# State-space blocks: one multiply for all tables, scans over four joined rows, and a later load of the gate bias

## The chip, the cores and the metric

The kernel runs on one core of a Trainium2 chip. Its engines are TensorE (PE in the profile; its weight loads are PEld), VectorE (DVE), ScalarE (ACT), GpSimd (POOL) and SyncE (SP), which here only starts DMA transfers. The metric is device time in microseconds (us); less is better.

## The reference

Two layers, one after the other, over 256 frames of width 2048. Each layer does this:

```
proj = x @ w_in                       # 2048 x 4096: q, k, v, u
attn = differential chunk-causal attention(q, k, v), 8 heads, normed per head
bu   = u @ B                          # per group of 16 channels: 64 complex states
h[t] = a * h[t-1] + bu[t]             # complex, |a| and angle per state, t = 0..255
y    = Re(C h) + d * u;  y = gelu(y)
ssm  = y * sigmoid(y @ glu_w + glu_b), normed per group
x    = layer_norm(alpha * x + concat(attn, ssm) @ w_out)
x    = layer_norm(alpha * x + relu(x @ w_up)^2 @ w_down)
```

There are 64 groups of 64 states. The change lies in the recurrence `h`, in the gelu behind it, and in where the gate's bias `glu_b` is loaded.

## The kernel before

**Matrix products.** Every large product is done three times in split fp32: weights arrive as 512 KB tiles `w` (two 128-row parts by 512 columns), ACT rounds one into `wh` (L185, by the helper on L155), DVE makes the rest `wl = w - wh` (L188, by the helper on L136), and PE multiplies hi by hi, hi by lo and lo by hi (L202). There are 714 such tiles, six buffers for `w` and four each for `wh` and `wl`.

**The mixer.** In each layer the projections, the attention heads, the state-space blocks, the gate and the output products run interleaved. A small planner (`Flow`) steps a clock of its own through tasks and writes out the order of PE's instructions; SP's order is the order in which the transfers are written. The order on DVE, ACT and POOL is chosen by the framework's list scheduler from its own model of times. So on the chip every engine works through a fixed list, and an instruction whose input is late holds up all that stand behind it on its engine.

**A state-space block** takes eight groups (four pairs `r`, two groups on the 128 partitions). Time is folded by two (`LC`), so a row has `NK` = 128 steps. There are eight blocks in a layer, 16 in all. For one block, POOL builds the tables `tab` (cosine and sine of the rotating angle, from `turn_on`, with products in `tm`), PE computes `X` = (real, imaginary) of the inputs, two pairs at a time into PSUM (L540), and DVE (`ssm_in`) turns X by the tables, scans the real and the imaginary part with the constant magnitude `magL`, and turns back. PE then forms `Y` from `h` (L581, behind the direct term of L572), and `ssm_out` applies the gelu on DVE and ACT. The tiles `wk` hold the four products, four buffers of 128x512. The planner puts the matmuls of Y `L_SCAN` = 12.5 us of its own clock behind those of X.

**Other tiles that the change touches.** `lb` (parameters B) and `ang` (angles) share the `wk` buffers during parameter preparation. `glub` is a tile of its own; its transfer stands on SP's queue among the first loads in the first layer (L1025) and ahead of the mixer in the second (L865). The pool `unit` has 18 tiles of 4 KB (`tile4k`), which nearly all other activations share.

Of the kernel before, what the change touches and what calls it, by code (L numbers as in the profile page):

```python
# [13 lines left out]
ALU = mybir.AluOpType  # L14
# [21 lines left out]
WB = 4  # L36
UN = 18
WS = 6
WK = 4
CHUNK = 64  # L40
ALPHA = (2.0 * DEPTH) ** 0.25
EPS = 1e-5
# [74 lines left out]
def trunk(ctx: ExitStack, tc: tile.TileContext, x, w_in, lambda_q1, lambda_k1, lambda_q2, lambda_k2,  # L117
# [51 lines left out]
    two = const.tile([P, 8], F32, name="two")  # L169
    for m in range(8):  # L170
        G.memset(two[:, m:m + 1], 2.0 ** m)
    mhalf = const.tile([P, 8], F32, name="mhalf")
    G.memset(mhalf, -0.5)

# [137 lines left out]
    def load_params(l):  # L312
        raw = ssm.tile([96, P], F32, tag="k0", name="prm", bufs=2)
        SY.dma_start(out=raw[0:32], in_=ssm_lambda_re[l].rearrange("(q g) p -> q (g p)", g=2))
        SY.dma_start(out=raw[32:64], in_=ssm_lambda_im[l].rearrange("(q g) p -> q (g p)", g=2))
        ld = ssm.tile([96, 2], F32, tag="ld", name="ld")
        SY.dma_start(out=ld[64:96], in_=ssm_log_dt[l].rearrange("(q g) -> q g", g=2))
        vec = ssm.tile([32, P], F32, tag="k0", name="vec", bufs=2)
        for i, v in enumerate((attn_norm_g, ssm_norm_g)):
            SY.dma_start(out=vec[8 * i:8 * i + 8], in_=v[l].rearrange("(b p) -> b p", p=P))  # L320
        for j in range(LC):
            SY.dma_start(out=vec[16:32].rearrange("x (r j c) -> x r j c", r=2, j=LC)[:, :, j],
                         in_=ssm_d[l].rearrange("(x r c) -> x r c", r=2, c=32))
        yield
        lb = [ssm.tile([P, NP_, GC], F32, tag="wk", name="lb", bufs=WK) for _ in range(2)]
        for a, v in zip(lb, (ssm_b_re, ssm_b_im)):
            SY.dma_start(out=a, in_=v[l].rearrange("(q g) p c -> (g p) q c", g=2))
            yield
        lc = [tile4k([P, 8, 2, HD], F32, "lc") for _ in range(2)]
        for i, v in enumerate((ssm_c_re, ssm_c_im)):  # L330
            for g in range(2):
                SY.dma_start(out=lc[i][:, :, g], in_=v[l].rearrange("(b g) c p -> (g c) b p", g=8))
                yield
        lq = ssm.tile([P, 4, HD], F32, tag="abc", name="lq")
        for i, v in enumerate((lambda_q1, lambda_k1, lambda_q2, lambda_k2)):
            SY.dma_start(out=lq[:, i], in_=v[l].partition_broadcast(P))
        return raw, ld, vec, lq, lb, lc

    def lay_params(fl, p, l, loaded):
# [26 lines left out]
        mag = t32("mag")[:, 0]  # L366
        G.tensor_tensor(out=mag, in0=ebase[:, 0:32], in1=tmp[:, 0], op=ALU.pow)

        rm, n = (ssm.tile([P, 8, NP_], F32, tag="wk", name="ang", bufs=WK) for _ in range(2))
        mul(rm, th.unsqueeze(1).to_broadcast([P, 8, NP_]), two.unsqueeze(2).to_broadcast([P, 8, NP_]))  # L370
        magic = 12582912.0
        ts(n, rm, 1.0 / (2.0 * math.pi), ALU.mult, magic, ALU.add)
# [33 lines left out]


        base_b, base_c = (tile4k([P, 2, NP_, GC], F32, "base") for _ in range(2))
        t1 = [ssm.tile([P, NP_, GC], F32, tag="wk", name="lb", bufs=WK) for _ in range(2)]
        for i in range(2):  # L410
            for h in range(2):
                yield fl.slot("tp")
# [5 lines left out]
                       v[64 * g:64 * g + 64, :, g], 1.0 - 2.0 * i, ALU.mult)  # L418
                give(L_EVAC)
        for o, (u, w, op) in enumerate(((0, 1, ALU.subtract), (1, 0, ALU.add))):  # L420
            mul(t1[0], lb[0], f[:, u].unsqueeze(2).to_broadcast([P, NP_, GC]))
            mul(t1[1], lb[1], f[:, w].unsqueeze(2).to_broadcast([P, NP_, GC]))
            tt_(base_b[:, o], t1[0], t1[1], op)
        p["base"], p["ab"] = (base_b, base_c), ab


# [100 lines left out]
    def ssm_in(fl, p, q, b, u):  # L527

        bT, k0, cx, tab, ready = q
        yield lambda: fl.now >= ready  # L530
        m1, m2, m3, m4 = (ssm.tile([P, 4, NK], F32, tag="wk", name="wk", bufs=WK) for _ in range(4))
        cos, sin = tab[:, 0], tab[:, 1]
        for hf in range(2):
            yield fl.slot("sx", 2)
            give = [fl.take("sx") for _ in range(2)]
            Xs = [ps_s.tile([P, 2, NK], F32, tag="sx", name="X") for _ in range(2)]
            for ri in range(2):
                for r, X in enumerate(Xs):
                    rows = slice(64 * r, 64 * r + 64)
                    TE.matmul(out=X[:, ri], lhsT=bT[rows, 2 * ri + hf], rhs=u[rows, hf], start=True, stop=True)  # L540
            fl.now += 0.87
            for r, X in enumerate(Xs, 2 * hf):
                mul(m1[:, r], X[:, 0], cos[:, r])
                mul(m2[:, r], X[:, 1], sin[:, r])
                mul(m3[:, r], X[:, 1], cos[:, r])
                mul(m4[:, r], X[:, 0], sin[:, r])
            for k, g in enumerate(give):
                g(L_X + 0.8 * k)
        add(m1, m1, m2)
        sub(m3, m3, m4)  # L550
        for g, s in ((m2, m1), (m4, m3)):
            for r in range(4):
                ml = p["magL"][:, 4 * b + r:4 * b + r + 1].to_broadcast([P, NK])
                V.tensor_tensor_scan(out=g[:, r], data0=ml, data1=s[:, r], initial=0.0,  # L554
                                     op0=ALU.mult, op1=ALU.add)
        mul(m1, m2, cos)
        mul(m3, m4, sin)
        sub(m1, m1, m3)
        mul(m2, m2, sin)
        mul(m4, m4, cos)  # L560
        add(m2, m2, m4)
        return m1, m2

    def ssm_out(fl, p, q, b, u, h):

        bT, k0, cx, tab, _ = q
        yield fl.slot("sx")
        give = fl.take("sx")
        Y = ps_s.tile([P, 2, NK], F32, tag="sx", name="Y")
        for hf in range(2):  # L570
            for r in range(2):
                TE.matmul(out=Y[64 * r:64 * r + 32, hf], lhsT=k0[:, hf, r], rhs=u[:, hf],  # L572
                          start=True, stop=False, skip_group_check=True)
            for ri in range(2):
                for i in (1, 0):
                    for r in range(2):
                        d, e = Y[64 * r + 32 * i:64 * r + 32 * i + 32, hf], h[ri][:, 2 * hf + r]
                        if i == 0:

                            d, e = d[:, 1:NK], e[:, 0:NK - 1]  # L580
                        TE.matmul(out=d, lhsT=cx[:, 2 * i + ri, 2 * hf + r].rearrange("p g c -> p (g c)"), rhs=e,  # L581
                                  start=(i == 1 and ri == 0), stop=(ri == 1), skip_group_check=True)
        fl.now += 1.5
        y, y2 = (ssm.tile([P, T], F32, tag="ge", name="ge", bufs=2) for _ in range(2))
        for hf in range(2):
            stt(y[:, hf * NK:(hf + 1) * NK], u[:, hf], p["vec"][:, 16 + 2 * b + hf:17 + 2 * b + hf], Y[:, hf],
                ALU.mult, ALU.add)
        give(L_EVAC)
        act(y2, y, AF.Square)
        ts(y2, y2, 0.044715, ALU.mult, 1.0, ALU.add)  # L590
        mul(y2, y2, y)
        act(y2, y2, AF.Tanh, scale=math.sqrt(2.0 / math.pi))
        stt(u.rearrange("p h k -> p (h k)"), y2, 1.0, y, ALU.add, ALU.mult)

# [260 lines left out]
    def mixer(l, p, xT, first):  # L855
# [4 lines left out]
        y_ev, mA_ev, mS_ev, (projected, g_ev) = events(8), events(8), events(2), events(2)  # L860
        uT = [tile4k([P, 8, NK], F32, "uT") for _ in range(2)]
        kT, qT, v = [None, None], [None, None], [None, None]
        gb = ssm.tile([P, SW], F32, tag="glub", name="glub")
        if l > 0:
            SY.dma_start(out=gb, in_=glu_b[l].partition_broadcast(P))  # L865
        loaded = []
        mA = [None, None]
        mS, glu_in, st = [], [], []
# [79 lines left out]
        def glu_inputs():  # L948
            yield both(*y_ev, projected)

            for i in range(2):
                st.append(tile4k([P, LC, NB], F32, "s"))
                for g in range(2):
                    yield fl.slot("tp")
                    give = fl.take("tp")
                    ps = transpose4(lambda n: uT[i][:, 4 * g + n])
                    fl.now += 0.44
                    act(st[i][:, :, 256 * g:256 * g + 256].rearrange("p j (x c) -> p j x c", c=32),
                        ps.rearrange("p n (r j c) -> p j (n r) c", r=2, j=LC))
                    give(L_EVAC)  # L960
            gS = Split("gS", 2)
            for i in range(2):
                for g in range(2):
# [49 lines left out]
        def main():  # L1013
            if l == 0:
                for i, test in enumerate(kproj(0)):
                    if i == 3:
                        with tc.manual_schedule(engines={ENG.Activation, ENG.DVE}):
                            turn_x(1)
                            first_w.append(wpair(w_in[0], 6, AW))
                        fl.now += 1.76  # L1020
                        for _ in range(5):
                            next(loading)
                    if i == 16:
                        loaded.append((yield from steps(loading, 0.0)))
                        SY.dma_start(out=gb, in_=glu_b[l].partition_broadcast(P))  # L1025
                    yield test
            else:
                yield from kproj(0)
# [105 lines left out]
```

## Time and profile before

| | |
|---|---|
| median of 3 runs | 2312.05 us (2311.9 to 2314.99) |
| the profiled execution | 2316.09 us |
| its span, first to last instruction | 2314.4 us |
| mean granted TensorE clock | 0.978 of full speed |

The profiled execution is 4.0 us above the median. All durations below are of this one execution. 1.7 us lie outside its span. The mixer of the first layer fills about 44 to 450 us of the span, that of the second 1180 to 1560; the MLP products lie between and behind them.

### The profile page before, as it was taken

The page shows a single profiled execution, that of the slowest core. Times are in us where ns is not written, and L with a number is a line of the kernel's source. Part 1 is how long each engine was busy: PE and PEld are TensorE (multiplying, and loading weights), DVE is VectorE, ACT ScalarE, POOL GpSimd, SP SyncE. Part 2 cuts the span into 40 slices and gives each one's busy share as a digit, 9 for nine tenths or more (in the row PEclk, how much of TensorE's full clock was granted, in tenths as well). Part 3 has the DMA queues.
Part 4 walks back from the last instruction along what each step waited for, and adds up shares of the span by engine and source line. Part 5 has one row for each costly group of instructions (what it writes and reads, how often), then busy time and mean ns, then how long its engine had stood idle before and what let it go on. Part 6 is the DMA issues. An engine that isn't in the chain of part 4 may idle for free.

```text
span 2314.4 us, 29243 instructions
## 1 busy us (share of the span) xinstructions
PE 2203.0 (95%) x10772; PEld 1781.9 (77%) x10772; DVE 1542.6 (67%) x2242; ACT 1076.9 (47%) x1527; POOL 330.4 (14%) x527
## 2 busy tenths in 40 slices
PE   8888979999999999999999799899999999999997
PEld 6766757788888878788878577677888888888886
DVE  4587887865565556656677978878565555556557
ACT  3444545354444444444445454644444444444443
POOL 1766310000000001700002842000000000000001
PEclk9988989999999999999999999999999999999999
DMA  8433424566766656566755343464666666565563
GB/s 257 136 112 100 146 73 145 191 189 188 202 192 187 207 180 187 165 199 183 239 155 154 116 128 111 134 193 147 199 183 190 192 188 190 185 197 184 183 201 144
DMA packets 227055, 396.54 MB, mean 171 GB/s; under 512 B 38336, under 2 KB 38496, under 8 KB 226912
## 3 DMA queue, kind: packets, MB, share of 16 engines
q1 hardware_dynamic: 226912, 394.68, 55.3%
q8 instruction: 85, 1.39, 0.2%
q14 instruction: 58, 0.48, 0.1%
HBM read 392.53 MB, written 2.10 MB: 171 GB/s over the span
## 4 chain that ended last, share of the span: by engine, by line
PE 77%; DVE 12%; POOL 3%; issue 3%; ACT 2%; DMA 1%; SPq 1%; DVEq 0%; ACTq 0%; POOLq 0%
PE acc L202 71%; DVE wk L136 3%; DVE wl L136 3%; POOL tm L136 2%; PE tp L237 2%; PE acc L757 2%; DVE wk L554 2%; DVE res L152 1%; ACT wh L155 1%; PE Y L581 1%; DMA w<-in_w_in 1%; PE X L540 1%; DVE res L136 0%; PE pT L642 0%; DVE st L712 0%
## 5 line engine op out<-in xcount | busy, mean ns | idle before, releaser
L136 DVE TENSOR_TENSOR wl<-w,wh 128x1024 fp32r<-128x1024 f32 x714 | 882.7, 1238 | 623.6 <-ACT wh L155 611.2
L155 ACT ACTIVATE wh<-w 128x1024 fp32r<-128x1024 f32 x714 | 755.6, 1060 | 844.0 <-PE acc L202 800.1
L202 PE MATMUL acc<-wh,xTh 128*128 128x512 f32 x1440 | 569.0, 402 | 8.8 <-ACT uraw L155 6.4
L202 PE MATMUL acc<-wl,xTh 128*128 128x512 f32 x1440 | 569.2, 395 | 2.9 <-DVE wl L136 2.9
L202 PE MATMUL acc<-wh,xTl 128*128 128x512 f32 x1440 | 567.8, 395 | 0.0
L202 PE MATMUL acc<-wh,hidh 128*128 128x512 f32 x1024 | 406.2, 397 | 4.9 <-DVE res L136 4.6
L202 PE MATMUL acc<-wh,hidl 128*128 128x512 f32 x1024 | 400.3, 391 | 0.0
L202 PE MATMUL acc<-wl,hidh 128*128 128x512 f32 x1024 | 399.2, 390 | 0.0
L202 PEld LDWEIGHTS acc<-wh,xTh 128*128 128x128 f32 x1440 | 275.6, 191 | 72.8 <-ACT uraw L155 7.3
L202 PEld LDWEIGHTS acc<-wl,xTh 128*128 128x128 f32 x1440 | 275.5, 191 | 60.1 <-DVE wl L136 6.4
L202 PEld LDWEIGHTS acc<-wh,xTl 128*128 128x128 f32 x1440 | 275.1, 191 | 58.2
L202 PEld LDWEIGHTS acc<-wh,hidh 128*128 128x128 f32 x1024 | 192.8, 188 | 44.4 <-DVE res L136 5.6
L202 PEld LDWEIGHTS acc<-wh,hidl 128*128 128x128 f32 x1024 | 192.6, 188 | 41.3
L202 PEld LDWEIGHTS acc<-wl,hidh 128*128 128x128 f32 x1024 | 192.9, 188 | 38.2
L136 DVE TENSOR_TENSOR res<-res,acc 128x512 f32<-128x512 f32 x288 | 196.4, 682 | 19.0 <-PE acc L202 17.2
L285 POOL TENSOR_TENSOR rs<-rs,mhalf 128x1 f32<-128x1 f32 x8 | 7.8, 973 | 1061.1 <-DVE rs L149 1061.1
L136 POOL TENSOR_TENSOR tm<-tab,pw 128x64 f32<-128x64 f32 (+2 forms) x192 | 123.6, 664 | 177.1 <-ACT tab L155 171.0
L155 ACT ACTIVATE raw<-acc 128x512 f32<-128x512 f32 x80 | 47.0, 588 | 57.2 <-PE acc L202 57.2
L136 DVE TENSOR_TENSOR wk<-X,tab 128x128 f32<-128x128 f32 x256 | 54.4, 278 | 17.6 <-PE X L540 16.3
L432 POOL TENSOR_TENSOR lel<-ebase,lsl 128x2 f32<-128x2 f32 x2 | 1.4, 710 | 448.1 <-DVE lsl L430 448.1
L136 POOL TENSOR_TENSOR tab<-tm 128x64 f32<-128x64 f32 (+2 forms) x96 | 61.5, 641 | 6.7
L202 PE MATMUL acc<-wh,mAh 128*128 128x512 f32 x128 | 52.9, 414 | 1.8 <-DVE res L152 1.8
(179 smaller groups left out, 2026.6 us busy)
## 6 DMA issues: line engine op xcount, KB each, us to landing
w<-in_w_up SPq DMA_DIRECT2D x256, 512.0 KB, 4.1
w<-in_w_down SPq DMA_DIRECT2D x256, 512.0 KB, 5.0
w<-in_w_in SPq DMA_DIRECT2D x128, 512.0 KB, 4.4
w<-in_w_out SPq DMA_DIRECT2D x64, 512.0 KB, 3.9
w<-in_glu_w SPq DMA_DIRECT2D x16, 512.0 KB, 3.7
gb<-in_ln_g SPq DMA_DIRECT2D x8, 512.0 KB, 8.8
gb<-in_ln_b SPq DMA_DIRECT2D x8, 512.0 KB, 10.0
out<-res SPq DMA_DIRECT2D x8, 256.0 KB, 2.1
```

Source lines behind the costliest of these rows:

```text
L136: (eng or V).tensor_tensor(out=out, in0=in0, in1=in1, op=op)
L152: V.scalar_tensor_tensor(out=out, in0=a, scalar=s, in1=b, op0=op0, op1=op1)
L155: S.activation(out=out, in_=in_, func=func, **kw)
L202: TE.matmul(out=acc, lhsT=a[:, c], rhs=b, start=(first and i == 0), stop=(last and i == 2))
L237: TE.transpose(ps[:, i], src(i), ident)
L285: G.tensor_tensor(out=self.rs, in0=self.rs, in1=mhalf[:, 0:1], op=ALU.pow)
L432: G.tensor_tensor(out=el, in0=ebase[:, 0:2], in1=sl, op=ALU.pow)
L540: TE.matmul(out=X[:, ri], lhsT=bT[rows, 2 * ri + hf], rhs=u[rows, hf], start=True, stop=True)
L554: V.tensor_tensor_scan(out=g[:, r], data0=ml, data1=s[:, r], initial=0.0, op0=ALU.mult, op1=ALU.add)
L581: TE.matmul(out=d, lhsT=cx[:, 2 * i + ri, 2 * hf + r].rearrange("p g c -> p (g c)"), rhs=e, start=(i == 1 and ri == 0), stop=(ri == 1), sk ...
L757: TE.matmul(out=acc[t], lhsT=(lo if i == LH else hi)[:, c], rhs=(wl if i == HL else wh)[:, k % 2], start=seen[t] == 0, stop=seen[t] == 3 * ...
```

## The change

In `ssm_in` the four separate products become one tile `wk` of [2, 2, 4, 128]: for each pair one multiply reads both parts of X (repeated for cosine and sine) and both tables (repeated for real and imaginary), 128x512 instead of four times 128x128. The eight scans of 128 steps become two of 512 steps over the four pairs of a part, one after the other in one row; the multiplier is a row `decay` that holds the magnitude at each step and zero at the first step of each pair, so that the state starts anew there. ACT fills this row once per block, in one of two constant tiles. The four multiplies after the scans become two of 128x1024. The gelu takes its constant 0.044715 into the scale of the square on ACT, and one DVE operation in place of two follows. The bias `glub` becomes a tile of the `unit` pool and is loaded when the gate's inputs are being laid out; its own 4 KB go, and the two decay tiles take 4 KB. `lb` and its temporaries share the one `wk` tile, and `ang` goes to the buffers of `tab`. The planner's lease of the second X buffer ends 0.3 us earlier.

```
+    decay = [const.tile([P, 4, NK], F32, name=f"decay{i}") for i in range(2)]
+    for d in decay:
+        G.memset(d[:, :, 0:1], 0.0)
...
-        lb = [ssm.tile([P, NP_, GC], F32, tag="wk", name="lb", bufs=WK) for _ in range(2)]
+        lb = ssm.tile([P, 4, NP_, GC], F32, tag="wk", name="lb")
...
-        rm, n = (ssm.tile([P, 8, NP_], F32, tag="wk", name="ang", bufs=WK) for _ in range(2))
+        ang = ssm.tile([P, 2, 8, NP_], F32, tag="tab", name="ang", bufs=2)
+        rm, n = ang[:, 0], ang[:, 1]
...
-        m1, m2, m3, m4 = (ssm.tile([P, 4, NK], F32, tag="wk", name="wk", bufs=WK) for _ in range(4))
-        cos, sin = tab[:, 0], tab[:, 1]
+        wk = ssm.tile([P, 2, 2, 4, NK], F32, tag="wk", name="wk")
...
             for r, X in enumerate(Xs, 2 * hf):
-                mul(m1[:, r], X[:, 0], cos[:, r])
-                mul(m2[:, r], X[:, 1], sin[:, r])
-                mul(m3[:, r], X[:, 1], cos[:, r])
-                mul(m4[:, r], X[:, 0], sin[:, r])
+                mul(wk[:, :, :, r], X.unsqueeze(1).to_broadcast([P, 2, 2, NK]),
+                    tab[:, :, r].unsqueeze(2).to_broadcast([P, 2, 2, NK]))
             for k, g in enumerate(give):
-                g(L_X + 0.8 * k)
-        add(m1, m1, m2)
-        sub(m3, m3, m4)
-        for g, s in ((m2, m1), (m4, m3)):
-            for r in range(4):
-                ml = p["magL"][:, 4 * b + r:4 * b + r + 1].to_broadcast([P, NK])
-                V.tensor_tensor_scan(out=g[:, r], data0=ml, data1=s[:, r], initial=0.0,
-                                     op0=ALU.mult, op1=ALU.add)
-        mul(m1, m2, cos)
-        mul(m3, m4, sin)
-        sub(m1, m1, m3)
-        mul(m2, m2, sin)
-        mul(m4, m4, cos)
-        add(m2, m2, m4)
-        return m1, m2
+                g(L_X + 0.5 * k)
+
+        dec = decay[b % 2]
+        act(dec[:, :, 1:NK], p["magL"][:, 4 * b:4 * b + 4].unsqueeze(2).to_broadcast([P, 4, NK - 1]))
+        s, h = wk[:, 0], wk[:, 1]
+        add(s[:, 0], s[:, 0], h[:, 1])
+        sub(s[:, 1], s[:, 1], h[:, 0])
+        flat = lambda a: a.rearrange("p r k -> p (r k)")
+        for i in range(2):
+            V.tensor_tensor_scan(out=flat(h[:, i]), data0=flat(dec), data1=flat(s[:, i]), initial=0.0,
+                                 op0=ALU.mult, op1=ALU.add)
+        mul(s, h, tab[:, 0].unsqueeze(1).to_broadcast([P, 2, 4, NK]))
+        mul(h, h, tab[:, 1].unsqueeze(1).to_broadcast([P, 2, 4, NK]))
+        sub(s[:, 0], s[:, 0], h[:, 1])
+        add(s[:, 1], s[:, 1], h[:, 0])
+        return s[:, 0], s[:, 1]
...
-        act(y2, y, AF.Square)
-        ts(y2, y2, 0.044715, ALU.mult, 1.0, ALU.add)
-        mul(y2, y2, y)
+        act(y2, y, AF.Square, scale=math.sqrt(0.044715))
+        stt(y2, y2, 1.0, y, ALU.add, ALU.mult)
...
-        gb = ssm.tile([P, SW], F32, tag="glub", name="glub")
-        if l > 0:
-            SY.dma_start(out=gb, in_=glu_b[l].partition_broadcast(P))
...
+            gb = tile4k([P, SW], F32, "glub")
+            SY.dma_start(out=gb, in_=glu_b[l].partition_broadcast(P))
             gS = Split("gS", 2)
...
-                        SY.dma_start(out=gb, in_=glu_b[l].partition_broadcast(P))
```

## Rows read from the trace of the kernel before

**Rows 1.** The page: busy time of each engine, then PE and DVE by slices.

```profile
PE 2203.0 (95%) x10772; PEld 1781.9 (77%) x10772; DVE 1542.6 (67%) x2242; ACT 1076.9 (47%) x1527; POOL 330.4 (14%) x527
PE   8888979999999999999999799899999999999997
DVE  4587887865565556656677978878565555556557
```

**Rows 2.** Windows: length, busy time of PE, PEld, DVE, ACT, POOL, granted clock, DMA.

```profile
108.00:140.00 32.00, 29.28 (x180) 21.61 (x180) 26.66 (x57) 14.83 (x24) 23.31 (x40) 0.89 0.36 109
260.00:300.00 40.00, 37.71 (x278) 28.28 (x277) 36.08 (x84) 20.13 (x41) 23.79 (x40) 0.96 0.44 129
300.00:340.00 40.00, 25.25 (x186) 18.44 (x185) 36.54 (x91) 14.25 (x41) 2.73 (x4) 0.80 0.25 82
500.00:840.00 340.00, 340.00 (x1532) 281.57 (x1531) 196.61 (x203) 154.58 (x166) 0.00 (x0) 1.00 0.65 193
1400.00:1457.00 57.00, 51.20 (x355) 38.22 (x353) 51.20 (x110) 22.74 (x39) 11.37 (x19) 0.97 0.42 131
```

**Rows 3.** The page: the chain that ended last, by engine and by line.

```profile
PE 77%; DVE 12%; POOL 3%; issue 3%; ACT 2%; DMA 1%; SPq 1%; DVEq 0%; ACTq 0%; POOLq 0%
PE acc L202 71%; DVE wk L136 3%; DVE wl L136 3%; POOL tm L136 2%; PE tp L237 2%; PE acc L757 2%; DVE wk L554 2%; DVE res L152 1%; ACT wh L155 1%; PE Y L581 1%; DMA w<-in_w_in 1%; PE X L540 1%; DVE res L136 0%; PE pT L642 0%; DVE st L712 0%
```

**Rows 4.** Waits: who waited for whom; us in total, times, longest.

```profile
ACT wh L155 <- PE acc L202: 800.1, 567, 6.5
PE Y L581 <- DVE wk L136: 20.6, 14, 5.3
DVE wk L136 <- PE X L540: 16.3, 11, 3.4
PE pT L635 <- DVE pe L152: 14.0, 8, 5.2
```

**Rows 5.** Groups by line and form: shape, count, busy us, mean ns, idle before.

```profile
L136 DVE TENSOR_TENSOR wk<-X,tab 128x128 f32<-128x128 f32 x256 | 54.4, 278 | 17.6 <-PE X L540 16.3 <-POOL tab L136 1.3
L554 DVE TENSOR_TENSOR_SCAN wk<-magL,wk 128x128 f32<-128x128 f32 x128 | 52.6, 476 | 0.1
L136 DVE TENSOR_TENSOR wk<-wk 128x512 f32<-128x512 f32 x64 | 45.3, 723 | 0.1
L136 DVE TENSOR_TENSOR wk<-wk,tab 128x512 f32<-128x512 f32 x64 | 43.4, 702 | 0.1
L155 ACT ACTIVATE raw<-raw 128x512 f32<-128x512 f32 x64 | 40.5, 632 | 2.0
```

**Rows 6.** DVE in order of time in the second layer: start, length, instructions merged.

```profile
1415.35 1.66 DVE L136 TENSOR_TENSOR wk<-X,tab 128x128 f32<-128x128 f32 x8
...
1422.28 1.23 DVE L136 TENSOR_TENSOR wl<-w,wh 128x1024 fp32r<-128x1024 f32 x1
1423.42 1.89 DVE L136 TENSOR_TENSOR wk<-wk,tab 128x512 f32<-128x512 f32 x3
...
1432.31 0.29 DVE L149 TENSOR_SCALAR ge<-ge 128x256 f32<-128x256 f32 x1 [0.48 <-ACT ge L155]
1432.64 0.42 DVE L136 TENSOR_TENSOR ge<-ge 128x256 f32<-128x256 f32 x1
...
1440.02 0.67 DVE L152 SCALAR_TENSOR_TENSOR res<-res,acc 128x512 f32<-128x512 f32 x1
1440.61 1.28 DVE L136 TENSOR_TENSOR wk<-wk 128x512 f32<-128x512 f32 x2
...
1442.13 2.56 DVE L554 TENSOR_TENSOR_SCAN wk<-magL,wk 128x128 f32<-128x128 f32 x8
```

**Rows 7.** Groups by form on DVE, 1400 to 1457 us.

```profile
L554 DVE TENSOR_TENSOR_SCAN wk<-magL,wk 128x128 f32<-128x128 f32 x16 | 5.2, 389 | 0.0
```

**Rows 8.** SP's queue in order of time, first layer.

```profile
33.97 0.43 SPq L1025 DMA_DIRECT2D glub<-in_glu_b  x1
34.50 10.83 SPq L180 DMA_DIRECT2D w<-in_w_in  x8
```

More of the change, by code (lines that the diff above doesn't have):

```diff
@@ L38 @@
 WS = 6
-WK = 4
 CHUNK = 64
@@ L324, in load_params @@
         yield
-        lb = [ssm.tile([P, NP_, GC], F32, tag="wk", name="lb", bufs=WK) for _ in range(2)]
-        for a, v in zip(lb, (ssm_b_re, ssm_b_im)):
-            SY.dma_start(out=a, in_=v[l].rearrange("(q g) p c -> (g p) q c", g=2))
+        lb = ssm.tile([P, 4, NP_, GC], F32, tag="wk", name="lb")
+        for a, v in enumerate((ssm_b_re, ssm_b_im)):
+            SY.dma_start(out=lb[:, a], in_=v[l].rearrange("(q g) p c -> (g p) q c", g=2))
             yield
@@ L408, in lay_params @@
         base_b, base_c = (tile4k([P, 2, NP_, GC], F32, "base") for _ in range(2))
-        t1 = [ssm.tile([P, NP_, GC], F32, tag="wk", name="lb", bufs=WK) for _ in range(2)]
+        t1 = lb[:, 2:4]
         for i in range(2):
@@ L420, in lay_params @@
         for o, (u, w, op) in enumerate(((0, 1, ALU.subtract), (1, 0, ALU.add))):
-            mul(t1[0], lb[0], f[:, u].unsqueeze(2).to_broadcast([P, NP_, GC]))
-            mul(t1[1], lb[1], f[:, w].unsqueeze(2).to_broadcast([P, NP_, GC]))
-            tt_(base_b[:, o], t1[0], t1[1], op)
+            mul(t1[:, 0], lb[:, 0], f[:, u].unsqueeze(2).to_broadcast([P, NP_, GC]))
+            mul(t1[:, 1], lb[:, 1], f[:, w].unsqueeze(2).to_broadcast([P, NP_, GC]))
+            tt_(base_b[:, o], t1[:, 0], t1[:, 1], op)
         p["base"], p["ab"] = (base_b, base_c), ab
```

## The prediction

> **What bounds the kernel now.** I read the page first. PE is busy for 95% of the span and DVE for 67% [rows 1], so PE is the bound as a whole, and DVE's time cannot count everywhere alike. The slices say where: in the MLP stretches PE stands at 9 and DVE at 5 or 6, while DVE's digits rise to 7, 8 and 9 in the two mixers, and there PE drops to 8 and 7 [rows 1]. The windows make that exact. From 500 to 840 us PE is busy for all 340 us while DVE works 196.6: an easier DVE changes nothing there. In four stretches of the mixers with state blocks DVE is busy 83% (26.66 of 32.00), 90%, 91% and 90% of the time, and PE loses 2.7, 2.3, 14.7 and 5.8 us [rows 2]; the granted clock is 0.80 to 0.97 there instead of 1.00, so that the busy part is slower too.
>
> The chain of waits gives the share of the end time: PE 77%, DVE 12%, POOL 3% [rows 3]. Of DVE's 12 points the state block has 3 (wk on L136) and 2 (the scans, L554). The table of waits names the place: PE's matmuls of Y waited 14 times for DVE's wk, 20.6 us in all, the longest 5.3 us [rows 4]. Behind the waiting Y stand the products of the weights, since PE works through one list. Attention's transposes lose 14.0 us more to DVE (pT after pe) [rows 4]; these are not the states' own results, but they stand in the same queue of DVE.
>
> So a shorter state block pays where Y waits, and through the shorter queue where pe is late. It pays nothing in the MLP.
>
> **What the change removes and adds on DVE, for one block.** I use the distance from one start to the next and not the length of a single operation, since neighbours overlap in the records.
>
> - *Turning X.* Eight multiplies of 128x128 take 1.66 us and one 0.278, so one start follows the other after (1.66 - 0.278)/7 = 0.197 us [rows 5, 6]. Sixteen are 3.15. The new ones are four of 128x512 with one operand in PSUM. The nearest row is an operation of that size with one operand in PSUM: res at 1440.02, next start at 1440.61, 0.59 us [rows 6]. Four are 2.36: 0.8 saved. Operands that repeat a row are not in the trace at this size; the lower bound is that each costs what its four parts cost (0.79), nothing saved.
> - *Sum and difference.* Two of 128x512 before and after, nothing.
> - *Scans.* Eight take 2.56 us; with the mean of 0.389 of this stretch for the last one, a start follows after (2.56 - 0.389)/7 = 0.31, and eight cost 2.48 [rows 6, 7]. Between starts, a multiply of 128x128 costs 0.197 and one of 128x512 0.61 (three take 1.89 us, two 1.28 [rows 6]), which is 0.06 fixed and 1.08 ns for a step ((0.61 - 0.197)/384). If the scan has the same fixed part, its step costs (0.31 - 0.06)/128 = 1.95 ns, and a scan of 512 costs 1.06 us, two 2.12: 0.36 saved. If instead its step costs 1.08 ns and the rest is fixed, a scan of 512 costs 0.72, two 1.43: 1.05 saved. At worst nothing is saved. I take 0.36, since a scan of 128 steps costs 0.11 us more than a multiply of the same size.
> - *Turning back.* Four multiplies of 128x512 are 2.44. Two of 128x1024 cost what wl costs, 1.14 from start to start (1422.28 to 1423.42), 2.28 [rows 6]: 0.16 saved. Two sums stay.
> - *Gelu.* A tensor_scalar goes: 0.33 from its start to the next (1432.31 to 1432.64) [rows 6]; the operation that replaces the multiply has the same shape and two operands as it. 0.33 saved. The scale on ACT's square is part of the same instruction, free.
>
> The sum is 0.8 + 0.36 + 0.16 + 0.33 = 1.6 us for a block, 26 us for 16. With the lower bounds it is 0.16 + 0.33 = 0.49, 8 us in all; with the quick scan 2.3, 37 us.
>
> [...]
>
> **What reaches the end.** The four groups of the states on DVE are busy 54.4 + 52.6 + 45.3 + 43.4 = 196 us [rows 5]. The chain holds 5% of 2314.4 us of them, 116 us [rows 3]: 0.59 of each saved microsecond lies on the path. 26 x 0.59 = 15 us; the bounds are 5 and 22. The other count agrees: 14 waits of Y at 1.5 us on average [rows 4], each reduced by at most the 1.6 us of its block, can give at most 20.6 us, and some of them are shorter than what the block saves. I take 13, since a short wait gives back only its own length. Where a stall of PE goes, PE's next inputs are due earlier: wh and wl, which ACT and DVE prepare ahead, and ACT then mostly waits for PE itself (800 us over 567 times [rows 4]), so it has room.
>
> **Edits off DVE.** The decay row is one ACT instruction of 128x508; the nearest row from SBUF is 128x512, 0.63 us [rows 5], 10 us in all on an engine that is busy for 47% [rows 1]. Its input exists since the parameters were laid out and its tile is free two blocks earlier, so it can stand far ahead of its scan: nothing, if the scheduler puts it there (the second rival says what it costs otherwise). The two memsets on POOL come at the start, ahead of its first work. Moving glub takes 0.5 us out of SP's first loads (33.97 to 34.50), directly ahead of eight weight tiles [rows 8], and its bytes from their way: 1 us gained, between nothing and 2. Its later load stands among the weight loads on SP at a time when DMA is 25 to 44% busy [rows 2]; the 18 unit tiles are then being given back by the projections, so I cost it at nothing. The lease that ends 0.3 us earlier lies inside one step of the planner (0.68 us) in most cases, so PE's order should stay the same but for rare places. One tile wk in place of four makes the next block's first multiply wait for the last matmul of Y that reads it; the next X stands behind that Y on PE anyway. lb and ang are used away from the blocks: nothing.
>
> The sum: -13 - 1 = -14 us. On the profiled 2316.09 that is 2302; the median is 4.0 below the profiled execution, so I state it for the median: 2312.05 - 14 = 2298 us.
>
> **Rivals.**
>
> *The wait is only handed on: no change.* PE's order is not planned anew, so DVE can have nothing to do until PE delivers the next X (already 16.3 us, 11 times [rows 4]), and another late input can hold PE at the same place. POOL's tables (2% of the chain, 46 us [rows 3]) are untouched, and DVE's list is sorted anew, so that a pe or wl may now come later than before. For it: every engine has a fixed list. Against it: from 300 to 340 us POOL works only 2.73 us and DVE 36.54 [rows 2], so there nothing but DVE is late. Gain 0 to 4 us, about 2310. Chance 0.19.
>
> *The decay row comes late: slower.* ACT's list is in order, and wh waits there for PE 1.4 us on average (800.1/567), 6.5 at most [rows 4]. If the row stands behind such a wh, the scans, all of DVE behind them, and Y wait. At 1.4 + 0.63 = 2.0 us for each block against 1.6 saved, 0.4 x 16 x 0.59 = 4 us are lost and the median is 2316; at the longest wait, (6.5 + 0.63 - 1.6) x 16 x 0.59 = 52, 2364. It decides from a delay of 1.6 us per block on. Against it: nothing forces it so late. Chance 0.07, most of it near 2318.
>
> *Longer operations hold POOL up: slower.* The scans' mean is 476 ns over all and 389 in this stretch [rows 5, 7]; what disturbs them are stretches with POOL at work (23.31 of 32 us from 108 to 140 [rows 2]). If DVE's longer operations slow POOL's products in return, its 46 us on the chain grow; it decides when they grow by 15/46, a third, and doubled they give 2312 + 46 - 14 = 2344. Against it: the elements that DVE reads are as many as before. [...] Chance 0.04.
>
> *The bias load blocks SP: slower.* If its unit tile is still in use, all weight loads stand behind it. PE has up to six w tiles ahead, so it decides only beyond some 10 us; about 2318. Chance 0.02.
>
> *The long operations are no cheaper.* With the lower bounds above 5 us are gained and with the bias load 6, 2306 to 2307: the edge of the forecast, counted in it.
>
> **How the numbers follow.** I call 0.2% (4.6 us) what a measurement of this kernel can tell from no change. The forecast, a gain of 5 to 28 us, has 0.68, the handed-on wait 0.19, the three slower ones 0.13. So faster 0.68, same 0.19, slower 0.13. Below, the quick scan gives 22 + 2 = 24 us, and if PE's clock no longer falls in stretches such as 300 to 340 (0.80 [rows 2]), some more: 2284. Above, the handed-on wait reaches to 2312. The range 2284 to 2312 leaves out the slower cases and the tail of the largest gains.
>
> **What the next profile would show.** The state multiplies on X: 64 of 128x512 at about 0.6 us from start to start. Scans: 32 of 512 steps at 1.06 us. DVE's busy time down by about 26 us, ACT's up by 10. Waits of PE's Y on wk well under 20.6 us. The MLP stretches unchanged. I am wrong in size if scans of 512 cost 0.72 or more than 1.3, and wrong in kind if Y's waits fall and others of PE (pT, X, uraw) grow by as much, or if a wait of DVE on decay appears.

## The result and the profile after

The changed kernel takes 2295.81 us (2294.69 to 2296.79, 4 runs), the kernel before 2313.52 us beside it. The ratio is 0.9924, interval [0.9908, 0.9939]: 17.7 us less. Forecast were 2298 us and a gain of 14.

The page of the changed kernel, busy time by engine, PE and DVE by slices, and the chain by engine and by line:

```profile
PE 2190.6 (96%) x10772; PEld 1775.5 (77%) x10772; DVE 1519.6 (66%) x1906; ACT 1082.4 (47%) x1543; POOL 346.5 (15%) x529
PE   8888979999999999999999789899999999999997
DVE  5586878855655556656677779777565565556557
...
PE 76%; DVE 9%; POOL 6%; issue 3%; ACT 2%; DMA 2%; SPq 1%; DVEq 0%; ACTq 0%; POOLq 0%
PE acc L204 70%; POOL tm L135 4%; DVE wk L135 2%; PE tp L239 2%; DVE wl L135 2%; PE acc L758 2%; DVE res L151 1%; DMA w<-in_w_in 1%; ACT wh L154 1%; POOL tab L135 1%; DVE wk L558 1%; POOL abc L135 1%; POOL fine L135 1%; PE X L543 1%; PE Y L583 0%
```

DVE executes 336 instructions less and is busy for 23.0 us less [rows 1]; 26 were forecast. The profiled span falls from 2314.4 to 2292.9 us, by 21.5 us. PE's busy time has 12.4 us of that, although it issues the same 10772 matmuls; its mean granted clock is 0.983 in place of 0.978, and half a per cent of 2203.0 is 11 us, so that by this estimate the clock can hold most of it. Its idle time has the other 9.1 (2314.4 - 2203.0 = 111.4 before, 2292.9 - 2190.6 = 102.3 after). In the chain DVE falls from 12 to 9%, and POOL rises from 3 to 6% [rows 3]. POOL itself is busy for 16.1 us more, although the change gives it only two short memsets.

PE's longest waits after the change (in total, times, longest):

```profile
PE pT L636 <- DVE pe L151: 10.2, 7, 2.6
PE tp L850 <- ACT raw L154: 8.6, 4, 6.6
PE tp L239 <- DVE o L135: 6.8, 3, 3.3
PE X L543 <- DVE ri L624: 6.1, 1, 6.1
...
PE X L543 <- DVE wk L135: 4.0, 1, 4.0
PE Y L583 <- DVE wk L135: 3.1, 4, 1.6
```

In the kernel before, three of these places had

```profile
PE tp L849 <- ACT raw L155: 3.7, 2, 3.2
...
PE tp L237 <- DVE o L136: 3.5, 1, 3.5
PE X L540 <- DVE ge L152: 3.4, 1, 3.4
```

The wait that the change aims at is nearly gone, 20.6 to 3.1 us [rows 4]. But idle time fell by 9.1 us and not by 17.5: the waits at X grew from 3.4 to 10.1 us, and those of tp for raw and o from 7.2 to 15.4. pT behind pe fell, from 14.0 to 10.2. The forecast's rival "handed on" was at work in part.

The state groups on DVE, by form (count, busy us, mean ns, idle before):

```profile
L135 DVE TENSOR_TENSOR wk<-wk 128x512 f32<-128x512 f32 x64 | 47.7, 783 | 0.4
L135 DVE TENSOR_TENSOR wk<-X,tab 128x512 f32<-128x512 f32 x64 | 41.1, 683 | 16.1 <-PE X L543 11.0 <-POOL tab L135 5.0
L558 DVE TENSOR_TENSOR_SCAN wk<-decay,wk 128x512 f32<-128x512 f32 x32 | 40.7, 1312 | 0.3
L135 DVE TENSOR_TENSOR wk<-wk,tab 128x1024 f32<-128x1024 f32 x32 | 40.7, 1271 | 0.5
```

They sum to 170 us in place of 196 [rows 5]. X and the turning back cost what the nearest rows said (0.68 and 1.2 us long when undisturbed, 0.6 and 1.14 from start to start). A scan of 512 steps has a median length of 1.218 us. Lengths overlap, so the forecast's costs are compared from start to start: two scans take 2.33 us where POOL is idle,

```profile
1420.00 2.33 DVE L558 TENSOR_TENSOR_SCAN wk<-decay,wk 128x512 f32<-128x512 f32 x2
```

and less one length of some 1.2 that leaves 1.13. This is near the slow case of the two that the forecast weighed (1.06) and far from the quick one (0.72).

### The profile page after: what moved, and what is told of

The parts are those of the page before. It is cut to its first block, busy times and chain, and to the rows that moved or that the text cites. A ratio compares the mean times of both kernels' runs of the same rounds, so it can differ in the third digit from the quotient of the medians.

```text
span 2292.9 us, 28919 instructions
## 1 busy us (share of the span) xinstructions
PE 2190.6 (96%) x10772; PEld 1775.5 (77%) x10772; DVE 1519.6 (66%) x1906; ACT 1082.4 (47%) x1543; POOL 346.5 (15%) x529
## 4 chain that ended last, share of the span: by engine, by line
PE 76%; DVE 9%; POOL 6%; issue 3%; ACT 2%; DMA 2%; SPq 1%; DVEq 0%; ACTq 0%; POOLq 0%
PE acc L204 70%; POOL tm L135 4%; DVE wk L135 2%; PE tp L239 2%; DVE wl L135 2%; PE acc L758 2%; DVE res L151 1%; DMA w<-in_w_in 1%; ACT wh L154 1%; POOL tab L135 1%; DVE wk L558 1%; POOL abc L135 1%; POOL fine L135 1%; PE X L543 1%; PE Y L583 0%
## 5 line engine op out<-in xcount | busy, mean ns | idle before, releaser
L135 DVE TENSOR_TENSOR res<-res,acc 128x512 f32<-128x512 f32 x288 | 196.8, 683 | 18.0 <-PE acc L204 16.2
L135 POOL TENSOR_TENSOR tm<-tab,pw 128x64 f32<-128x64 f32 (+2 forms) x192 | 130.5, 699 | 149.2 <-ACT tab L154 143.1
L135 POOL TENSOR_TENSOR tab<-tm 128x64 f32<-128x64 f32 (+2 forms) x96 | 67.9, 707 | 6.8
L135 DVE TENSOR_TENSOR hidl<-tp,hidh 128x512 fp32r<-128x512 f32 x64 | 44.0, 688 | 14.8 <-ACT hidh L154 14.8
## 6 DMA issues: line engine op xcount, KB each, us to landing
gb<-in_ln_b SPq DMA_DIRECT2D x8, 512.0 KB, 10.2
```

The source lines that it names most:

```text
L135: (eng or V).tensor_tensor(out=out, in0=in0, in1=in1, op=op)
```

## The experiments

Each kernel ran four to eleven times beside the kernel before; the ratio is to that one. Its median was 2314.89, 2313.85 and 2313.95 us in the three groups.

**Is it the states or PE's order?** The change holds a number of the planner, the lease of the second X buffer. The forecast took it for nothing, except in rare places, where it would change the order of PE's list. The first kernel is the changed one with the old lease, the second the old one with the new lease.

```
# e1: after          -                g(L_X + 0.5 * k)
                     +                g(L_X + 0.8 * k)
# e2: before         -                g(L_X + 0.8 * k)
                     +                g(L_X + 0.5 * k)
```

> The changed kernel with the planner's lease of the second X buffer as before (0.8 in place of 0.5). In the mixers PE's list of instructions is then that of the kernel before; only DVE, ACT, POOL and SP have the change. Theory A (the shorter state work on DVE gives the gain): 12 to 20 us below the kernel before, as the changed kernel. Theory B (the new order of PE's list gives it): less than 5 us below the kernel before.

> The kernel before with the lease of the changed one (0.5), so with the changed kernel's order of PE in the mixers and the old state work on DVE. Theory A: within 5 us of the kernel before, Y's waits on wk stay near 20 us. Theory B: 10 us or more below the kernel before.

Measured: e1 2303.44 us, ratio 0.9951 [0.9937, 0.9965], 11.4 us less; e2 2306.63 us, 0.9961 [0.9948, 0.9973], 8.3 us less. Neither theory holds alone: the new lease gives 8 (with a new order of PE's list, and the lists of the other engines sorted anew for it), the rest of the change 9 to 11, and together 18. In e2 the state work is as before, and yet PE waits less for it; its waits:

```profile
PE pT L635 <- DVE pe L152: 16.4, 11, 4.1
PE Y L581 <- DVE wk L136: 13.6, 11, 2.2
...
PE tp L237 <- DVE o L136: 5.9, 1, 5.9
```

Y waits 13.6 us, longest 2.2, in place of 20.6 and 5.3 [rows 4]. The long one stood at the end of the first layer's state blocks. There the kernel before has

```profile
330.20 0.44 PE L237 MATMUL tp<-ident,o 128*128 128x128 f32 x2 [3.54 <-DVE o L136]
330.57 0.64 PE L572 MATMUL Y<-uT,k 128*32 128x128 f32 x4
336.51 0.65 PE L581 MATMUL Y<-wk,cx 128*32 128x128 f32 x8 [5.29 <-DVE wk L136]
```

and e2 has

```profile
331.91 0.69 PE L237 MATMUL tp<-ident,o 128*128 128x128 f32 x2 [5.85 <-DVE o L136]
332.53 0.43 PE L572 MATMUL Y<-uT,k 128*32 128x128 f32 x2
332.54 0.43 PE L581 MATMUL Y<-wk,cx 128*32 128x128 f32 x2
332.76 1.28 PE L581 MATMUL Y<-wk,cx 128*32 128x128 f32 x18
```

(lines of PE in order of time; in brackets the idle time before). In front of that Y, PE now stands longer for attention's o, 5.85 in place of 3.54 us, and wk is there when it comes to Y: at this place the two waits fall from 8.83 to 5.85 us together, 3.0 of the 8.3. Where the rest lies was not followed further.

**Bias load, gelu, and both with the lease.** The diffs are the hunks of the change for glub and gelu, applied to the kernel before; the third kernel has both and the new lease, so that only the operations on the states separate it from the changed kernel.

> The kernel before with the bias load moved and nothing else. By the prediction's step: 1 us below the kernel before (0 to 2). Rival: the load among the gate's weights holds SP's queue up, and it is 1 to 4 us above.

> The kernel before with the gelu in one DVE operation less and nothing else: 0.33 us per block, 5.3 us of DVE. Theory A with the chain's share: 3 us below the kernel before (1 to 5). Rival: more, 5 us or above, since this operation stands between two steps of ACT on the way to the next blocks and the gate.

> The kernel before with the new lease, the moved bias load and the shorter gelu, but with the old operations on the states (16 multiplies, 8 scans, 4 multiplies). PE's list is that of the changed kernel. The changed kernel is 18 us below the kernel before, the new lease alone 8. If the state operations are worth what the old lease left of the gain (theory A), this one is 9 to 12 us below the kernel before. Rival: merging the state operations gives nothing by itself, and this one is 16 us or more below.

Measured: the bias load 2316.1 us, 1.0011 [1.0002, 1.0019], 2.3 us more; the gelu 2311.27, 0.9988 [0.9980, 0.9997], 2.6 us less; all but the states 2307.2, 0.9970 [0.9959, 0.9982], 6.7 us less. The three alone sum to -8.3 + 2.3 - 2.6 = -8.6. The state operations are then worth the rest, (0.9970 - 0.9924) x 2314 = 10.6 us. In the trace of e7, Y waits for wk 14.1 us, in that of the changed kernel 3.1:

```profile
PE Y L581 <- DVE wk L136: 14.1, 9, 2.7
```

The moved load shows no gain; its loss has the sign of the rival's side, and is no larger than what a new sorting of the lists moves by itself (below). Whether it holds up another transfer is not shown.

**Which of the state operations?** From the changed kernel, I undid the multiplies on X, the scans, both, and the multiplies behind the scans.

```
# e3, e9   -  mul(wk[:, :, :, r], X.unsqueeze(1)..., tab[:, :, r].unsqueeze(2)...)
           +  for c in range(2):
           +      for ri in range(2):
           +          mul(wk[:, c, ri, r], X[:, ri], tab[:, c, r])
# e4, e9   -  act(dec[:, :, 1:NK], ...)     and the two scans of 512
           +  for r in range(4):
           +      ml = p["magL"][:, 4 * b + r:4 * b + r + 1].to_broadcast([P, NK])
           +      V.tensor_tensor_scan(out=h[:, i, r], data0=ml, data1=s[:, i, r], ...)
# e10      -  mul(s, h, cos); mul(h, h, sin); sub; add
           +  mul(s[:, 0], h[:, 0], cos); mul(s[:, 1], h[:, 1], sin); sub(s[:, 0], s[:, 0], s[:, 1])
           +  mul(h[:, 0], h[:, 0], sin); mul(h[:, 1], h[:, 1], cos); add(s[:, 1], h[:, 0], h[:, 1])
```

> The changed kernel with the sixteen multiplies of 128x128 on X for each block in place of four of 128x512; PE's list is the same as in the changed kernel. They cost 0.8 us more of DVE per block, 13 us in all. Theory A with the chain's share of 0.59: 8 us above the changed kernel (5 to 11). Rival: what counts is only whether Y's waits vanish, and the rest of the gain is not proportional: 0 to 3 us above it.

> The changed kernel with eight scans of 128 steps with the constant magnitude in place of two of 512, and so without the decay row and its instruction on ACT. By DVE alone (2.48 against some 2.3 us per block) 3 us of work come back, 2 us above the changed kernel. Rival: the decay row makes ACT wait for the scans two blocks back (12.5 us, 8 times, in the changed kernel's waits), so that without it the time is 3 to 6 us below the changed kernel.

> The changed kernel with both the old sixteen multiplies on X and the old eight scans; of the state operations only the two multiplies of 128x1024 and the single tile wk stay. PE's list is that of the changed kernel but for places in the MLP. Theory C (the gain saturates: as long as a part of the work is gone, Y's waits are gone, and the first part to be undone costs little): 4 to 8 us above the kernel with only the scans undone, so 0 to 3 us above the changed kernel. Theory D (neither of the two merges has a part in it, the gain is in the multiplies behind the scans and the tile): within 2 us of the kernel with only the scans undone.

> The changed kernel with four multiplies of 128x512 behind the scans in the order of before (real part complete after three operations) in place of two of 128x1024. By DVE's time 0.16 us per block, 2.5 us, so 1 to 2 us above the changed kernel (theory C). Theory D: 6 us or more above it, up to the 11 us that the state operations gave.

| | us | ratio, interval | DVE busy | POOL busy | PE idle | Y waits for wk |
|---|---|---|---|---|---|---|
| changed kernel | 2295.81 | 0.9924 [0.9908, 0.9939] | 1519.6 | 346.5 | 102.3 | 3.1 |
| e3, X undone | 2298.73 | 0.9927 [0.9914, 0.9939] | 1531.0 | 347.0 | 99.7 | 4.9 |
| e4, scans undone | 2292.91 | 0.9903 [0.9889, 0.9916] | 1531.0 | 335.2 | 95.4 | 8.3 |
| e9, both undone | 2298.3 | 0.9938 [0.9925, 0.9950] | 1536.6 | 335.6 | 98.6 | 9.4 |
| e10, last multiplies undone | 2291.94 | 0.9908 [0.9894, 0.9921] | 1525.0 | 347.1 | 101.2 | 4.9 |
| e7, all states as before | 2307.2 | 0.9970 [0.9959, 0.9982] | 1537.9 | 333.1 | 105.7 | 14.1 |

(PE idle is span less busy time.) The parts don't add. The merged X is worth 0.7 us with the new scans (0.9927 - 0.9924), and 8.1 us with the old ones (0.9938 - 0.9903): with the old scans it pays what the forecast's rate gives (13 us x 0.59 = 7.6), and where the new scans have taken their part, nothing that can be seen. That is the direction of theory C; each of the two differences is uncertain by some 4 us, so the size is not settled. The merged scans are no gain: without them DVE works 11.4 us more, and the time is not longer but 4.9 us lower (by the ratios, whose intervals overlap a little). The last multiplies too are rather better apart, by 3.7 us, with intervals that overlap by half. That leaves the step from e7 to e9, 7.4 us by the ratios with only 1.3 us less of DVE, to what e9 still has of the change: multiplies of 128x1024, the single tile wk, ang and lb in other buffers, and lists of DVE, ACT and POOL sorted anew for them. Theory D's expectation for e9 fell, but so did that of e10 under both theories; no run takes this step apart.

**Does the decay row cost time on ACT?** In the changed kernel, a fill writes the tile that the scans two blocks earlier read, and ACT waits for these scans. The waits:

```profile
ACT decay L154 <- DVE wk L558: 12.5, 8, 4.1
```

```
# e11: one tile      -  dec = decay[b % 2]      +  dec = decay[0]
# e12: fill on DVE   -  act(dec[:, :, 1:NK], ...)  +  V.tensor_copy(out=dec[:, :, 1:NK], in_=...)
```

> The changed kernel with one decay tile in place of two, so that every fill waits for the scans of the block ahead; nothing else. If ACT's waits for the scans (12.5 us in 8 fills) are what the decay row costs: these waits grow towards 20 us or more and the time rises 3 to 5 us above the changed kernel. Rival: ACT has room and the time stays within 2 us.

> The changed kernel with the decay row filled by DVE in place of ACT: ACT waits for no scan any more, DVE gets one copy of 128x508 per block, 0.3 to 0.6 us, 5 to 10 us in all. If ACT's waits cost 4 us: 1 to 3 us below the changed kernel in spite of the copy. Rival, ACT's waits cost nothing: 1 to 5 us above it.

Measured: e11 2297.29 us, 0.9929 [0.9916, 0.9943]; e12 2294.7 us, 0.9917 [0.9903, 0.9930]. The edit of e11 moved the waits only from 12.5 to 16.2 us, and the time by 1 us; e12 took them away at 8.4 us more of DVE's time (1528.0 against 1519.6) and stands 1.6 us below by the ratios. Both signs fit a cost of ACT's waits, both sizes are inside the intervals. What the waits cost stays open: e12 gives 1.6 us if the copy's 8.4 us of DVE cost nothing, and 6.6 if they cost the forecast's rate of 0.59.

**How much does a new sorting move by itself?**

> The changed kernel with the imaginary part first in the sum and difference and in the scans: the same operations, the same PE list, only the list scheduler sorts anew. If re-sorting alone is harmless: within 2 us of the changed kernel. Rival: it moves the time by 3 to 6 us either way, and then differences of that size between the other kernels can't be put down to the operations themselves.

The edit swaps the two lines behind X and runs the scans as (1, 0). Measured: 2294.3 us, 0.9912 [0.9898, 0.9925], 2.8 us below the changed kernel by the ratios. So 3 us is what I hold for indistinct among these kernels; it rests on this one sorting, and others may move more or less.

## Why the prediction was right, and where its steps were not

**The bound and the place: right.** The gain lies in the mixers. Windows of the changed kernel, with the columns of [rows 2]:

```profile
108.00:140.00 32.00, 30.61 (x209) 23.21 (x209) 29.88 (x33) 16.38 (x30) 28.74 (x35) 0.95 0.43 132
300.00:340.00 40.00, 28.76 (x202) 20.10 (x203) 32.02 (x65) 20.59 (x61) 2.56 (x4) 0.84 0.10 27
500.00:840.00 340.00, 340.00 (x1528) 281.57 (x1527) 193.54 (x197) 156.18 (x169) 0.00 (x0) 1.00 0.65 194
```

In the MLP PE is full before and after. In the stretch from 300 to 340 PE works 28.76 in place of 25.25 us (the work in it is not the same, since everything stands earlier).

**DVE's saving and the rate: right as a sum, not shown as a mechanism.** 26 us were forecast, 23.0 measured; at 0.59 the gelu's 5.3 us are worth 3 (2.6 measured; the scale on ACT's square cost nothing that shows, 412 ns on average for ACT's operations of the gelu against 410 before), and the states' 21 us some 10 after the discount (10.6 measured, e7 against the changed kernel). But of these 10.6 us 7.4 lie in the step from e7 to e9, where DVE works only 1.3 us less; there little of the time can come from DVE's saved work, and that the number agrees is in part luck. The rate is an average at best: X pays 8.1 us with the old scans and 0.7 with the new ones.

**The scans' term: not borne out.** The step said two scans save 0.36 us per block, 5.8 in all, and so 3 us at the end. (Two scans at the quick case's 0.72 are 1.44 us and not the 1.43 of that working; nothing hangs on it.) Where POOL is idle, eight short scans take 2.56 us and two long ones 2.33: 0.23 us per block, 3.7 in all. DVE's busy time of scans fell by 52.6 - 40.7 = 11.9 us; the rest, 8.2, is what the short scans lost beside POOL beyond what the long ones do (all 52.6 us are 11.6 more than 16 times 2.56, all 40.7 are 3.4 more than 16 times 2.33). And yet undoing it lengthens nothing. The trace shows a price elsewhere, the third rival's: POOL. In the seven kernels with scans of 512 POOL is busy for 345.9 to 350.5 us, in the kernel before and in e2, e4, e5, e7 and e9 for 329.5 to 335.6. In the first layer both engines are at work at the same time. There DVE has in the changed kernel

```profile
113.68 2.65 DVE L558 TENSOR_TENSOR_SCAN wk<-decay,wk 128x512 f32<-128x512 f32 x2
...
118.31 3.31 DVE L135 TENSOR_TENSOR wk<-wk,tab 128x1024 f32<-128x1024 f32 x2
...
155.44 1.29 DVE L135 TENSOR_TENSOR wk<-X,tab 128x512 f32<-128x512 f32 x2 [1.06 <-PE X L543]
```

and POOL at the same time

```profile
113.98 1.26 POOL L135 TENSOR_TENSOR tab<-tm 128x128 f32<-128x128 f32 x1
115.33 1.98 POOL L135 TENSOR_TENSOR tm<-tab,pw 128x256 f32<-128x256 f32 x2
...
119.07 3.03 POOL L135 TENSOR_TENSOR tm<-tab,pw 128x256 f32<-128x256 f32 x2
...
155.75 1.18 POOL L135 TENSOR_TENSOR tm<-tab,pw 128x256 f32<-128x256 f32 x2
```

A sum of 128x128 takes 1.26 us wholly beside the long scans, and 0.46 in the kernel before at 114.84, beside eight multiplies of X (lines below). The same two products of 128x256 take 1.98 us where they begin beside the long scans, and 3.03 beside the two multiplies of 128x1024, which are themselves stretched (3.31 us in place of some 2.3). They take 1.18 beside two multiplies of 128x512, which are longer than a short scan (0.68 us against some 0.39) but read one operand, X, from PSUM. So it is not length alone that counts; whether the operand in PSUM is what spares POOL was not shown, since no run varies that alone. In the kernel before, and in e4, the eight short scans at this place were stretched instead, and POOL's pair ran in 1.30. The kernel before has

```profile
114.06 1.66 DVE L136 TENSOR_TENSOR wk<-X,tab 128x128 f32<-128x128 f32 x8
...
117.06 5.39 DVE L554 TENSOR_TENSOR_SCAN wk<-magL,wk 128x128 f32<-128x128 f32 x8
```

```profile
114.84 0.46 POOL L136 TENSOR_TENSOR tab<-tm 128x128 f32<-128x128 f32 x1
...
117.53 1.30 POOL L136 TENSOR_TENSOR tm<-tab,pw 128x256 f32<-128x256 f32 x2
```

and e4

```profile
114.37 5.43 DVE L558 TENSOR_TENSOR_SCAN wk<-magL,wk 128x128 f32<-128x128 f32 x8
```

```profile
115.21 1.30 POOL L135 TENSOR_TENSOR tm<-tab,pw 128x256 f32<-128x256 f32 x2
```

So at this place the long scans turn a loss of DVE (5.43 us in place of 2.56 [rows 6], against 2.65 in place of 2.33) into one of POOL. That POOL's 11 us take back what DVE saves fits e4, but it is not shown: e4 also frees ACT, and POOL's share of the chain is 6% in e4 as in the changed kernel. e12 frees ACT and keeps the long scans; POOL is busy for 347.4 us there, so its rise belongs to the scans and not to ACT's fill, but its time lies between the two, 1.6 us below the changed kernel and 3.2 above e4 by the ratios, too close to decide. What the long scans cost at the end stays open.

**PE's order: the step that failed.** "The lease that ends 0.3 us earlier lies inside one step of the planner (0.68 us) in most cases" was costed at nothing. It is worth 8.3 us (e2), nearly half of the gain. In e1, where PE has the order that the forecast took for granted, the gain is 11.4 us.

**The bias load: not borne out**, 2.3 us lost in place of 1 gained (e5), a difference at the edge of what can be told. The step took 0.5 us out of SP's first loads. In e5, which moves this load alone, the weight loads that stood behind it start at 34.65 us, no earlier than the 34.50 of the kernel before [rows 8]. In the changed kernel they start at 33.07, but there the load just ahead of them, of lambda_k, took 0.43 us to issue, in place of 1.45 in the kernel before and 1.37 in e5; so that start cannot be put down to the bias.

**The decay row on ACT:** 9.8 us of ACT's time as forecast; the row was not late for its scans (DVE waits for no decay in the table), but its fill waits for older scans, which the forecast had not named.

The total of 14 came close to 17.7 in part by luck: an order that was not counted (8.3) stood against terms that were too kind (the bias load, the scans).

## What to carry to other kernels

Where each engine works through a fixed list, cost a change of the planner's numbers by itself: 0.3 us in a lease was worth nearly as much here as the rewrite of the operations (8.3 and 10.6 us). A rate such as "0.59 of each saved microsecond is on the path" need not hold for each part, so undo the parts one at a time and in pairs. Long scans on VectorE were not free for GpSimd beside them (346 to 350 us of its busy time, 330 to 336 without them); of the kernels that ran, the old scans with all else changed (2292.91 us) and the changed kernel with the last multiplies apart (2291.94 us) are the fastest, both below the changed kernel by little more than the measurement can tell.

## What the runs showed of the hardware

In the changed kernel a scan of 512 steps cost about 1.8 times as much as a multiply of the same shape: a median of 1.218 us against 0.68 us for 128x512. Two GpSimd products of 128x256 took 1.18 us beside VectorE multiplies with one operand in PSUM, 1.30 beside short scans, 1.98 where they began beside long scans, and 3.03 beside multiplies of 128x1024 with both operands in SBUF. Eight short scans took 5.39 us beside GpSimd and 2.56 without it; two long ones 2.65 and 2.33. PE's busy time is no fixed sum: with the same 10772 matmuls, PE's busy time was 2188.0 us in e10 and 2203.0 us in the kernel before, at a mean granted clock of 0.983 and 0.978.
